# Layer 0's first strips: where shift is computed, and the order of loads and copies around them

## The chip, the core and the metric

The kernel runs on one NeuronCore of one Trainium2 chip. It is one launch. The metric is the time of that launch in microseconds (us) on the device, as the median of several runs. A core has five engines, each with a queue of its own that it works through in order: TensorE (PE, matrix products into PSUM), VectorE (DVE), ScalarE (ACT), GpSimd (POOL) and SyncE (SP), which here only issues DMAs. ACT issues a few DMAs too.

## The reference, cut to what the change touches

Two layers act on one sequence of 1024 tokens with 1024 channels, in float32. Layer 0 is a block-diagonal state-space mixer (S5), layer 1 forgetting attention. Only layer 0's beginning matters here:

```python
def reference(x, c, ...):                       # layer 0
    shift, scale, gate = split(silu(c) @ mod_w + mod_b, 3)
    h = rms(x, norm_g) * (1.0 + scale) + shift
    y = s5_mixer(h, w_in, log_dt, A, B, C, D, w_glu, b_glu, w_out)
    x = x + gate * y                            # then layer 1

def s5_mixer(h, ...):
    u, z = split(h @ w_in, 2)                   # 1024 channels each
    dt = exp(log_dt)
    abar = exp(A_re * dt) * (cos(A_im * dt) + i sin(A_im * dt))
    bb = (abar - 1) / A * B                     # complex, 64 groups
    s[t] = abar * s[t-1] + bb @ u[t]            # per group: 64 states, 16 channels
    y = real(C @ s) + D * u
    y = gelu(y); y = y * sigmoid(y @ w_glu + b_glu); y = y * silu(z)
    return y @ w_out
```

## The kernel before

All of it stands in one function, `trunk`. Products in near-float32 accuracy are made from three products of parts: an operand is split into a high half (a copy in the type fp32r, on ACT, L93) and a low half (the remainder, on DVE, L101), and high times high, low times high and high times low are added in PSUM (`in_part`, L258 to L265).

**Strips.** The product of h with `w_in` is made in strips of 128 output channels. Strip e of u has 1024 x 128 weights, read by `weight_strip` (L83) into the one buffer `w_raw` and split into `w_hi` and `w_lo`, of which there are two each. A strip is made of three chunks of tokens (`CH`): chunk 0 of 512 tokens, chunk 1 of 256, and chunk 2, the short one (`128x258` in the profile), of 256 tokens and two further columns, which hold shift and so give the strip's bias `bi`. In a chunk eight k-tiles by three products are added in a PSUM bank. The part of h without shift is x scaled per channel (`aH`, `aL`, written at L295 and L296 as x arrives); the two shift columns are added to the last tile of tokens (L339, L340). The rms factor is applied to the result: `et` = bank times `q2` (L361, DVE); then `ut` = `et` + `bi` in another order (L378, ACT), and `ut`, of which there is one buffer, is stored to memory as `u_d` (L381, SP).

**What is made first.** `scale` comes with x, k-tile by k-tile (L253 and L288). Strips 0 and 1 (chunks 0 and 1) run with it on PE (`u01`, L310 to L313). Strip 2's weights `raw2` (L315) are split into `w2` in a pool of its own. Shift is silu(c) times `mod_sh`, read as eight tiles `mws` of 512 KB (L324): four of them lie in the ring `xw`, four in the places of `ut`, `bbs`, `x1m` and `x2m`, which so are free only once shift has been computed. The products `psh` (L280 and L283: groups of four products of 32 rows, made side by side) come in two halves of 512 channels, each from all eight tiles. They are copied to `shr` (L332) and turned into columns by eight small products `pm` (L335). Only with these columns can a short chunk start.

**The states' tables.** From A and dt come angles and their sines and cosines (`th`, `ang`, L413 to L437), the powers `pwr`, `pwi` and their signed copies `rvr`, `rvi` (L472, L473), and the coefficients `cr`, `ci`, `cis`. B and C are read twice in two orders: `bb`, `bbs`, `x1m`, `x2m` (L508, L509). `bb` is multiplied by the coefficients, its two halves of partitions are exchanged by DMAs of ACT (`bbs<-bb`, L522), and from `bb`, `bbs` and powers come `wm`, whose transposition `pin` (L595) opens the first group's work on PE. `turn_in` makes `pin`, `taps` the product `pk` (L607), and strips 4 to 7 and those of z are laid among the groups' work.

**What sets the order.** The program is handed to a scheduler which sorts each engine's instructions by a model of their times. `tc.issue_after(m)` adds one constraint: what is written under it comes behind instruction m. Before the change, `mws` come behind the last load of x (L323), the whole chain from `th` on stands behind `last_lo`, the last low half of the shift columns (the gate at L408), and the loads of B and C stand behind the last load of `mws` (L506). The lines that set this for shift are:

```python
psh = [pj.tile([P, HL], F32, name=f"psh{i}", tag="pj") for i in range(2)]
for r in range(2):
    for i in range(2):
        quarters(psh[i], [cs[:, k] for k in range(4 * r, 4 * r + 4)],
                 [t[:, HL * i:HL * i + HL] for t in mws[4 * r:4 * r + 4]], r == 0, r == 1)
```

The tag `pj` is a ring of two PSUM banks that the chunks use too.

## Time and profile before

| what | us |
|---|---|
| median of 3 runs | 1240.18 |
| lowest and highest | 1239.35, 1244.92 |
| the profiled execution's own time | 1235.67 |
| its span, from the first to the last instruction | 1233.9 |
| its time outside the span | 1.77 |

The profile is taken from one execution by the hardware's profiler, and times within it count from the span's start. A row of a timeline holds start, duration, engine, line, operation, output <- inputs, size and count, and in brackets how long the engine had been idle and which instruction ended that. A name without a number stands for all buffers of that name; `u` is a chunk's PSUM bank. The granted clock is the share of full speed at which PE ran. Line numbers are those of the kernel before.

### The profile page before, as it was taken

Reading aid. Unit: us, or ns where it says so; the run is one execution under the profiler, and the core shown is the slowest. Engines: PE = TensorE matmul, PEld = TensorE weight load, DVE = VectorE, ACT = ScalarE, POOL = GpSimd, SP = SyncE. Lnnn points to the kernel's source line nnn. Section 1 sums busy time; section 2 is a strip of 40 time slices with the busy share of each in tenths; the row PEclk is TensorE's granted clock in tenths of the full one; section 3 lists DMA queues with packets and bytes.
Section 4 is the critical chain, followed back from the end, with each engine's and each line's share of the span. In section 5 each row is a group of like instructions: output and inputs, shape, how many; then the busy total and the mean of one; then the engine's idle time right before and its main releaser. Section 6 shows DMA issues by size and latency. Waiting matters only on the chain.

```text
span 1233.9 us, 20697 instructions
## 1 busy us (share of the span) xinstructions
PE 1162.0 (94%) x7594; PEld 1015.9 (82%) x7594; DVE 838.7 (68%) x1708; ACT 606.0 (49%) x1141; POOL 368.5 (30%) x569
## 2 busy tenths in 40 slices
PE   7897999997999998899999999999999999999898
PEld 5586888887878776699989999997888888888686
DVE  7377999894678867856355673448787877887421
ACT  6474667564634422432213352227776777786310
POOL 4000000000000021730043464536675766664100
PEclk8997999998999999999999999999999999999999
DMA  9734556576695697238454159426887969771242
GB/s 353 214 96 119 164 149 174 158 189 192 227 306 184 206 314 259 67 112 259 175 183 171 70 169 190 137 103 153 155 156 135 169 123 172 143 148 27 94 162 77
DMA packets 113333, 205.30 MB, mean 166 GB/s; under 512 B 17072, under 2 KB 58160, under 8 KB 111696
## 3 DMA queue, kind: packets, MB, share of 16 engines
q1 hardware_dynamic: 86272, 161.44, 40.8%
q0 software_dynamic: 24960, 37.75, 17.9%
q10 hardware_dynamic: 2000, 4.79, 1.7%
q8 instruction: 60, 0.98, 0.4%
q14 instruction: 41, 0.34, 0.1%
HBM read 146.47 MB, written 46.20 MB: 156 GB/s over the span
## 4 chain that ended last, share of the span: by engine, by line
PE 56%; DVE 17%; DMA 15%; ACT 4%; issue 4%; SPq 2%; POOL 2%; ACTq 0%; POOLq 0%; DVEq 0%
PE tkps L889 17%; PE zb L112 6%; PE pj_f L112 5%; DMA modw<-modw 5%; PE tp L1081 4%; PE ov L1088 3%; PE u L263 3%; PE ov L1087 3%; PE sp L1048 3%; PE z L263 2%; PE sp L1049 2%; DMA v_d<-vt 2%; PE pj_g L112 2%; PE f L112 2%; DVE modw L132 1%
## 5 line engine op out<-in xcount | busy, mean ns | idle before, releaser
L889 PE MATMUL tkps<-wvh,aH 128*128 128x256 f32 (+1 forms) x768 | 220.7, 287 | 5.7 <-DVE vt L901 2.9
L889 PE MATMUL tkps<-wvh,aL 128*128 128x256 f32 (+1 forms) x768 | 216.8, 282 | 0.0
L889 PE MATMUL tkps<-wvl,aH 128*128 128x256 f32 (+1 forms) x768 | 216.7, 282 | 0.0
L889 PEld LDWEIGHTS tkps<-wvh,aH 128*128 128x128 f32 x768 | 145.1, 189 | 8.2 <-DVE vt L901 3.9
L889 PEld LDWEIGHTS tkps<-wvl,aH 128*128 128x128 f32 x768 | 145.5, 189 | 0.3 <-issue 0.2
L889 PEld LDWEIGHTS tkps<-wvh,aL 128*128 128x128 f32 x768 | 145.0, 189 | 0.3 <-issue 0.2
L1083 ACT ACTIVATE pth<-tp 128x512 fp32r<-128x512 f32 (+1 forms) x192 | 87.1, 488 | 61.0 <-PE ov L1087 35.4
L1056 ACT ACTIVATE pr<-pr,mx 128x128 f32<-128x128 f32 (+7 forms) x128 | 98.9, 773 | 23.0 <-DVE mx L1053 22.5
L1058 POOL TENSOR_SCALAR pr<-pr,sm 128x128 f32<-128x128 f32 (+7 forms) x128 | 96.1, 759 | 41.9 <-DVE sm L1057 41.8
L1084 DVE TENSOR_TENSOR ptl<-tp,pth 128x512 fp32r<-128x512 f32 (+1 forms) x192 | 101.2, 551 | 8.7 <-ACT pth L1083 8.0
L93 ACT ACTIVATE w_hi<-w_raw 128x1024 fp32r<-128x1024 f32 x49 | 51.6, 1054 | 79.9 <-PE pj_f L112 35.8
L1053 DVE CUSTOM_DVE_ANT_0 pr<-sp,fb 128x512 f32<-128x512 f32 (+3 forms) x128 | 72.8, 570 | 22.2 <-PE tp L1081 20.0
L1087 PE MATMUL ov<-pth,vhl 128*128 128x256 f32 x320 | 84.7, 297 | 0.1
L1081 PE MATMUL tp<-ident,pr 128*128 128x128 f32 x576 | 83.1, 273 | 0.0
L912 ACT ACTIVATE hsq<-tkps 128x256 f32<-128x256 f32 x64 | 24.5, 383 | 117.0 <-PE tkps L889 109.8
L1088 PE MATMUL ov<-ptl,vhl 128*128 128x256 f32 x320 | 80.1, 284 | 0.2 <-DVE ptl L1084 0.2
L132 DVE CUSTOM_DVE_ANT_0 modw<-modw,c_b 128x1024 f32<-128x1024 f32 x48 | 58.4, 1220 | 31.2 <-DMA modw<-modw 31.0
L1048 PE MATMUL sp<-kk,qs 128*128 128x256 f32 (+2 forms) x192 | 74.7, 389 | 2.9 <-DVE mx L1053 1.9
L1081 PEld LDWEIGHTS tp<-ident,pr 128*128 128x128 f32 x576 | 65.4, 141 | 7.1 <-POOL pr L1058 0.5
L832 POOL TENSOR_TENSOR sq<-sq,sq 128x512 f32<-128x512 f32 x12 | 19.7, 1645 | 170.8 <-ACT sq L828 170.8
L914 POOL TENSOR_SCALAR hms<-hms 128x4 f32<-128x4 f32 x64 | 16.9, 264 | 174.5 <-DVE hms L913 171.0
L915 POOL TENSOR_TENSOR hms<-hms,nhalf 128x4 f32<-128x4 f32 x64 | 66.4, 1039 | 5.0
(339 smaller groups left out, 3299.8 us busy)
## 6 DMA issues: line engine op xcount, KB each, us to landing
modw<-modw SPq DMA_DIRECT2D x48, 512.0 KB, 5.2
kk<-k_d POOLq DMA_DIRECT2D x32, 512.0 KB, 6.8
wvr<-kvq_w SPq DMA_DIRECT2D x12, 1024.0 KB, 5.3
w_raw<-a_w_in SPq DMA_DIRECT2D x16, 512.0 KB, 4.9
v_d<-vt SPq DMA_DIRECT2D x32, 256.0 KB, 2.8
fb<-f_d SPq DMA_DIRECT2D x16, 512.0 KB, 9.0
vhl<-v_d POOLq DMA_DIRECT2D x16, 512.0 KB, 9.6
qs<-q_d POOLq DMA_DIRECT2D x32, 256.0 KB, 8.4
```

Of the source, the lines that this page charges most:

```text
L112: T.matmul(ps, w[wt][:, k, :], act[at][k][half], start=(k == k0 and n == 0), stop=(k == k1 and n == 2))
L132: V.tensor_tensor_reduce(out=mw, in0=mw, in1=c_b, scale=1.0, scalar=0.0, op0=ALU.mult, op1=ALU.add, accum_out=mod[:, n:n + 1])
L889: T.matmul(ps[:, 0:nv], at, wt[:, k, 0:nv], start=(n == 0), stop=(n == 3 * KT - 1))
L1048: T.matmul(sp[:, 0:wm_], qsl, kk[:, 0, lo:lo + wm_], start=True, stop=False)
L1053: V.tensor_tensor_reduce(out=pr[:, lo:hi], in0=sp[:, 0:w_], in1=fb[:, lo:hi], scale=1.0, scalar=3e38 if m0 is None else m0, op0=ALU.add, o ...
L1056: S.activation(pr[:, 0:nk], pr[:, 0:nk], AF.Exp, scale=-1.0, bias=mx, accum_out=sm)
L1058: G.tensor_scalar(out=pr[:, 0:nk], in0=pr[:, 0:nk], scalar1=sm, scalar2=0.0, op0=ALU.mult, op1=ALU.add)
L1081: T.transpose(out=tp[:, b, :], in_=prs[qi][:, P * (b0 + b):P * (b0 + b) + P], identity=ident)
L1083: S.activation(pth[:, 0:m, dst], tp[:, 0:m, :], AF.Copy)
L1084: V.tensor_tensor(out=ptl[:, 0:m, dst], in0=tp[:, 0:m, :], in1=pth[:, 0:m, dst].bitcast(F32), op=ALU.subtract)
L1087: T.matmul(ov, vhl[:, b, :], pth[:, b - b0, :], start=(b == 0), stop=False)
L1088: end = T.matmul(ov, vhl[:, b, :], ptl[:, b - b0, :], start=False, stop=(b == nb - 1)).ins
```

## The change

The diff has seven edits, all in layer 0's beginning.

- The warm-up products `wu` are 32 instead of 18.
- The load of strip 2's weights stands right behind the last load of x. The eight loads of `mws` follow it one behind another, in the order 4, 5, 6, 7, 0, 1, 2, 3.
- The two halves of shift are made behind chunk 0 and chunk 1 of strip 2, each as a whole from all eight tiles, in a PSUM bank with a tag of its own, `psh`, in the pool `pj0`. There is one such bank, so the second half waits for the copy of the first.
- `pm` and the shift columns come behind both halves.
- Strip 3's weights are read behind the last load of `mws`, in a call of their own, and the loads of B and C come behind that load (`w3_load`).
- The gate of the chain from `th` on is `lo_end`, the last low half of x, instead of `last_lo`.
- The copies of `x1m` and `x2m` come behind strip 3's high half, the products of `bb` and `bbs` behind its low half (`w3_parts`).

```diff
@@ -80,9 +80,11 @@
         fb_t = ctile([NH, 1], "fb_t")
 
 
+        wdma, parts = [], [None] * 2
+
         def weight_strip(src, shape, l_eng=None, pool=None):
             raw = (pool or wpool).tile(shape, F32, name="w_raw", tag="w_raw", bufs=2 if pool else 1)
-            Q.dma_start(out=raw, in_=src)
+            wdma.append(Q.dma_start(out=raw, in_=src).ins)
             hi = wpool.tile(shape, F32R, name="w_hi", tag="w_hi")
             lo = wpool.tile(shape, F32R, name="w_lo", tag="w_lo")
             split(raw, hi, lo, None, l_eng)
@@ -90,15 +92,15 @@
 
         def copy_on(eng, o, i):
             if eng is S:
-                S.activation(o, i, AF.Copy)
+                return S.activation(o, i, AF.Copy)
             elif eng is G:
                 G.tensor_scalar(out=o, in0=i, scalar1=1.0, scalar2=0.0, op0=ALU.mult, op1=ALU.add)
             else:
                 V.tensor_copy(out=o, in_=i)
 
         def split(x, hi, lo, h_eng=None, l_eng=None):
-            copy_on(h_eng or S, hi, x)
-            (l_eng or V).tensor_tensor(out=lo, in0=x, in1=hi.bitcast(F32), op=ALU.subtract)
+            h = copy_on(h_eng or S, hi, x)
+            parts[:] = h, (l_eng or V).tensor_tensor(out=lo, in0=x, in1=hi.bitcast(F32), op=ALU.subtract)
 
 
         def act_tiles(more=0):
@@ -265,7 +267,7 @@
                 return m
 
             wu = pj.tile([P, HL], F32, name="wu", tag="pj")
-            for _ in range(18):
+            for _ in range(32):
                 T.matmul(wu[:, 0:P], onesm, onesm, start=True, stop=True)
             o32 = xp.tile([P, P], F32, name="o32")
             G.memset(o32, 1.0 / 32)
@@ -293,8 +295,8 @@
                 for i in range(2):
                     hi, xs = act[0][k][i][:, 0:HL], xt[:, HL * i:HL * i + HL]
                     S.activation(hi, xs, AF.Copy, scale=s_a[:, k:k + 1])
-                    V.scalar_tensor_tensor(out=act[1][k][i][:, 0:HL], in0=xs, scalar=s_a[:, k:k + 1], in1=hi.bitcast(F32),
-                                           op0=ALU.mult, op1=ALU.subtract)
+                    lo_end = V.scalar_tensor_tensor(out=act[1][k][i][:, 0:HL], in0=xs, scalar=s_a[:, k:k + 1],
+                                                    in1=hi.bitcast(F32), op0=ALU.mult, op1=ALU.subtract).ins
                 sq = xp.tile([P, L], F32, name="sqx", tag="sqx", bufs=4)
                 sq_end = S.activation(sq, xt, AF.Square).ins
                 sqs.append(sq)
@@ -312,33 +314,18 @@
                     for c in range(2):
                         in_part(u01[e][c], w01[e], c, (k,))
             raw2 = wpool.tile([P, KT, P], F32, name="w_raw", tag="w_raw", bufs=1)
-            Q.dma_start(out=raw2, in_=a["a_w_in"][2])
+            with tc.issue_after(last_x):
+                last_w = Q.dma_start(out=raw2, in_=a["a_w_in"][2]).ins
             w2 = [xp.tile([P, KT, P], F32R, name=f"w2{i}", tag=f"w2{i}") for i in range(2)]
             split(raw2, *w2)
 
-            mws = []
-            for k in range(KT):
+            mws = [None] * KT
+            for k in (4, 5, 6, 7, 0, 1, 2, 3):
                 pool, tag = ((s5, "ut"), (s5, "bbs"), (s5, "x1m"), (s5, "x2m"))[k - 4] if k >= 4 else (xp, "xw")
-                mws.append(pool.tile([P, D], F32, name="mws", tag=tag, bufs=7 if pool is xp else 1))
-                with tc.issue_after(last_x):
+                mws[k] = pool.tile([P, D], F32, name="mws", tag=tag, bufs=7 if pool is xp else 1)
+                with tc.issue_after(last_w):
                     last_mod = Q.dma_start(out=mws[k], in_=a["mod_sh"][k])
-            psh = [pj.tile([P, HL], F32, name=f"psh{i}", tag="pj") for i in range(2)]
-            for r in range(2):
-                for i in range(2):
-                    quarters(psh[i], [cs[:, k] for k in range(4 * r, 4 * r + 4)],
-                             [t[:, HL * i:HL * i + HL] for t in mws[4 * r:4 * r + 4]], r == 0, r == 1)
-            shr = xp.tile([P, D], F32, name="shr", tag="sqx", bufs=4)
-            for i in range(2):
-                S.activation(shr[:, HL * i:HL * i + HL], psh[i], AF.Copy)
-            pm = pj0.tile([P, NG], F32, name="pm", tag="dps")
-            for k in range(KT):
-                T.matmul(pm[:, 2 * k:2 * k + 2], shr[:, P * k:P * k + P], o32[:, 0:2], start=True, stop=True)
-            for k in range(KT):
-                hi, b = act[0][k][1][:, HL:], vec["modb"][:, k:k + 1]
-                m = pm[:, 2 * k:2 * k + 2]
-                S.activation(hi, m, AF.Identity, bias=b)
-                last_lo = V.scalar_tensor_tensor(out=act[1][k][1][:, HL:], in0=m, scalar=b, in1=hi.bitcast(F32),
-                                                 op0=ALU.add, op1=ALU.subtract).ins
+                    last_w = last_mod.ins
             with tc.issue_after(sq_end):
                 S.preload_act_table_set("natural_log_exp_and_others")
             vx = xp.tile([P, L], F32, name="vx")
@@ -397,15 +384,37 @@
                     yield m
 
             u2 = []
+            shr = xp.tile([P, D], F32, name="shr", tag="sqx", bufs=4)
             for c in range(2):
-                u2.append(u_norm(chunk(w2, c, "u2")[0], c, xp))
+                ps, m = chunk(w2, c, "u2")
+                u2.append(u_norm(ps, c, xp))
+                with tc.issue_after(m):
+                    psh = pj0.tile([P, HL], F32, name=f"psh{c}", tag="psh")
+                    for r in range(2):
+                        quarters(psh, [cs[:, k] for k in range(4 * r, 4 * r + 4)],
+                                 [t[:, HL * c:HL * c + HL] for t in mws[4 * r:4 * r + 4]], r == 0, r == 1)
+                S.activation(shr[:, HL * c:HL * c + HL], psh, AF.Copy)
+            pm = pj0.tile([P, NG], F32, name="pm", tag="dps")
+            for k in range(KT):
+                T.matmul(pm[:, 2 * k:2 * k + 2], shr[:, P * k:P * k + P], o32[:, 0:2], start=True, stop=True)
+            for k in range(KT):
+                hi, b = act[0][k][1][:, HL:], vec["modb"][:, k:k + 1]
+                m = pm[:, 2 * k:2 * k + 2]
+                last_hi = S.activation(hi, m, AF.Identity, bias=b).ins
+                last_lo = V.scalar_tensor_tensor(out=act[1][k][1][:, HL:], in0=m, scalar=b, in1=hi.bitcast(F32),
+                                                 op0=ALU.add, op1=ALU.subtract).ins
             for e in range(U_FIRST):
-                for _ in u_strip(e, *((w01[e], u01[e]) if e < 2 else (w2, (), u2) if e == 2 else ())):
+                if e == 3:
+                    with tc.issue_after(last_mod.ins):
+                        w3 = weight_strip(a["a_w_in"][3], [P, KT, P])
+                    w3_parts = [p.ins for p in parts]
+                for _ in u_strip(e, *((w01[e], u01[e]) if e < 2 else (w2, (), u2) if e == 2 else (w3,))):
                     pass
+            w3_load = wdma[-1]
 
 
             gate = ExitStack()
-            gate.enter_context(tc.issue_after(last_lo))
+            gate.enter_context(tc.issue_after(lo_end))
 
             th = tmp.tile([P, 8, NG], F32, name="th")
             mul(th[:, 0], aim, dt)
@@ -503,21 +512,23 @@
             bbs = s5.tile([P, NG, GC], F32, name="bbs", tag="bbs")
             x1m = s5.tile([P, NG, GC], F32, name="x1m", tag="x1m")
             x2m = s5.tile([P, NG, GC], F32, name="x2m", tag="x2m")
-            with tc.issue_after(last_mod.ins):
+            with tc.issue_after(w3_load):
                 for o, i0, i1 in ((bb, "B_re", "B_im"), (bbs, "B_im", "B_re"), (x1m, "C_re", "C_im"), (x2m, "C_im", "C_re")):
                     Q.dma_start(out=o[0:64], in_=a[i0])
                     Q.dma_start(out=o[64:128], in_=a[i1])
-            S.activation(x1m, x1m, AF.Copy, scale=sg_pm)
-            S.activation(x2m, x2m, AF.Copy, scale=-1.0)
 
             cis = tmp.tile([P, NG], F32, name="cis")
             S.activation(cis, ci, AF.Copy, scale=sg_mp)
+            with tc.issue_after(w3_parts[0]):
+                S.activation(x1m, x1m, AF.Copy, scale=sg_pm)
+                S.activation(x2m, x2m, AF.Copy, scale=-1.0)
             shb = [P, NG // 2, GC]
             for gs in (slice(0, 32), slice(32, 64)):
                 crb, cib = (t[:, gs].unsqueeze(2).broadcast_to(shb) for t in (cr, cis))
-                mul(bbs[:, gs], bbs[:, gs], cib)
-                mul(bb[:, gs], bb[:, gs], crb)
-                tt(bb[:, gs], bb[:, gs], bbs[:, gs], ALU.add)
+                with tc.issue_after(w3_parts[1]):
+                    mul(bbs[:, gs], bbs[:, gs], cib)
+                    mul(bb[:, gs], bb[:, gs], crb)
+                    tt(bb[:, gs], bb[:, gs], bbs[:, gs], ALU.add)
                 for hh in range(2):
                     S.dma_start(out=bbs[64 * hh:64 * hh + 64, gs], in_=bb[64 - 64 * hh:128 - 64 * hh, gs])
 
```

How the order of the instructions moves is seen at three places. The first is PE between strip 1 and strip 2. `msy` are the rms sums, `u_1_190` and `u_0_525` are banks of chunks, `psh` shift's halves, `pm` the columns' bank. Before, all of shift's products and half of `pm` stand ahead of strip 2's first chunk:

```order
L309 MATMUL msy_344<-mq,o_210 128x512
L280 MATMUL psh_465<-mws,cs 32x512
L283 MATMUL psh_465<-mws,cs 32x512 x3
L280 MATMUL psh_466<-mws,cs 32x512
L283 MATMUL psh_466<-mws,cs 32x512 x3
L280 MATMUL psh_465<-mws,cs 32x512
L283 MATMUL psh_465<-mws,cs 32x512 x3
L280 MATMUL psh_466<-mws,cs 32x512
L283 MATMUL psh_466<-mws,cs 32x512 x3
L335 MATMUL pm<-o_210,shr 128x2 x4
L263 MATMUL u_0_525<-aH_0_150,w_445 128x512
```

Now strip 2's chunk 0 comes straight behind strip 1, and the first half, `psh_521`, stands within its chunk 1 (`u_1_531`):

```order
L265 MATMUL u_1_531<-aH_1_161,w_459 128x256
L282 MATMUL psh_521<-mws,cs 32x512
L285 MATMUL psh_521<-mws,cs 32x512 x3
L282 MATMUL psh_521<-mws,cs 32x512
L285 MATMUL psh_521<-mws,cs 32x512 x3
L265 MATMUL u_1_531<-aL_1_177,w_459 128x256
```

and the second, `psh_558`, behind that chunk, followed by all eight `pm` and the short chunks of strips 0 and 1 (`u_2_595`, `u_2_633`):

```order
L265 MATMUL u_1_531<-aH_1_165,w_460 128x256
L282 MATMUL psh_558<-mws,cs 32x512
L285 MATMUL psh_558<-mws,cs 32x512 x3
L282 MATMUL psh_558<-mws,cs 32x512
L285 MATMUL psh_558<-mws,cs 32x512 x3
L399 MATMUL pm<-o_224,shr 128x2 x8
L265 MATMUL u_2_595<-aH_1_151,w_hi 128x258
L265 MATMUL u_2_633<-aH_1_151,w_hi 128x258
```

So the first half moved behind chunk 0 and most of chunk 1, the second stands eight chunk products further on, and the columns come in one piece. The short chunks of strips 0 and 1, which before came mostly one after the other, are now laid into each other to their end.

The second place is SP's queue behind the last load of x (`xt`). `fb_t` and `dsk` are small constants. Before:

```order
L288 DMA xt<-xT 128x1024
L324 DMA mws<-mod_sh 128x1024 x4
L508 DMA bb<-B_re 64x1024
L315 DMA w_raw<-a_w_in 128x1024
L509 DMA bb<-B_im 64x1024
L324 DMA mws<-mod_sh 128x1024
L527 DMA fb_t<-f_bias 16x1
L324 DMA mws<-mod_sh 128x1024
L528 DMA dsk<-D 128x16
L324 DMA mws<-mod_sh 128x1024 x2
L85 DMA w_raw<-a_w_in 128x1024
L508 DMA x2m<-C_im 64x1024
```

Now:

```order
L290 DMA xt<-xT 128x1024
L318 DMA w_raw<-a_w_in 128x1024
L327 DMA mws<-mod_sh 128x1024 x8
L538 DMA fb_t<-f_bias 16x1
L539 DMA dsk<-D 128x16
L87 DMA w_raw<-a_w_in 128x1024
L517 DMA bb<-B_re 64x1024
L518 DMA bb<-B_im 64x1024
L517 DMA x2m<-C_im 64x1024
L518 DMA x2m<-C_re 64x1024
L517 DMA bbs<-B_im 64x1024
L518 DMA bbs<-B_re 64x1024
```

The load of strip 2's weights moved ahead of all of `mws`, `bb` moved out from among them, and the loads into `mws`' former places follow strip 3's weights.

The third place is ACT from strip 3's split on: `x1m` and `x2m` are C's tiles, `ut` the strips' outputs, `bbs<-bb` the exchange of halves. Before, `x2m` and `x1m` stood right behind `shr` and ahead of the shift columns:

```order
L332 ACTIVATE shr<-psh_465 128x512
L332 ACTIVATE shr<-psh_466 128x512
L511 ACTIVATE x2m<-x2m 128x1024
L510 ACTIVATE x1m<-x1m,sg_pm 128x1024
L339 ACTIVATE aH_1_151<-pm,vecs 128x2
L339 ACTIVATE aH_1_153<-pm,vecs 128x2
```

Now they stand behind strip 3's split and ahead of strip 0's `ut`, and the exchanges are issued on either side of strip 1's:

```order
L403 ACTIVATE aH_1_165<-pm,vecs 128x2
L95 ACTIVATE w_hi<-w_raw 128x1024
L523 ACTIVATE x1m<-x1m,sg_pm 128x1024
L524 ACTIVATE x2m<-x2m 128x1024
L365 ACTIVATE ut<-et,bi 128x32x8
L365 ACTIVATE ut<-et,bi 128x64x8
L365 ACTIVATE ut<-et,bi 128x32x8
L95 ACTIVATE w_hi<-w_raw 128x1024
L533 DMA bbs<-bb 64x512 x2
L365 ACTIVATE ut<-et,bi 128x32x8
L365 ACTIVATE ut<-et,bi 128x64x8
L365 ACTIVATE ut<-et,bi 128x32x8
L533 DMA bbs<-bb 64x512 x2
```

## The prediction

> **What bounds the kernel now.** I read the page first, then a table of windows cut where TensorE (PE) changes its work, then the waits of the first 140 us, then single rows. The page says that PE is the engine to follow: busy 94% of the span, and most of the chain that ended last.
>
> ```profile
> span 1233.9 us, 20697 instructions
> PE 1162.0 (94%) x7594; PEld 1015.9 (82%) x7594; DVE 838.7 (68%) x1708; ACT 606.0 (49%) x1141; POOL 368.5 (30%) x569
> PE 56%; DVE 17%; DMA 15%; ACT 4%; issue 4%; SPq 2%; POOL 2%; ACTq 0%; POOLq 0%; DVEq 0%
> ```
>
> The windows (from:to, length, busy time of PE, PEld, DVE, ACT, POOL with counts, granted clock, DMA share, GB/s) show where PE stands still:
>
> ```profile
> 24.94:41.89 16.95, 16.92 (x92) 12.02 (x92) 10.43 (x18) 11.55 (x17) 0.00 (x0) 1.00 1.03 320
> 41.89:47.02 5.13, 0.01 (x1) 0.03 (x1) 4.05 (x6) 3.25 (x6) 0.00 (x0) 0.95 1.01 373
> 47.02:52.93 5.91, 5.91 (x41) 2.22 (x41) 0.96 (x2) 1.19 (x2) 0.00 (x0) 0.75 0.03 12
> 52.93:62.47 9.54, 9.54 (x58) 8.27 (x57) 0.00 (x0) 1.87 (x2) 1.00 (x2) 1.00 0.74 167
> 62.47:77.45 14.98, 12.22 (x97) 11.79 (x97) 10.14 (x30) 8.85 (x23) 0.00 (x0) 1.00 0.21 71
> 77.45:94.87 17.42, 17.38 (x96) 14.70 (x96) 14.87 (x45) 13.10 (x31) 0.00 (x0) 1.00 0.48 143
> 94.87:103.79 8.92, 0.00 (x0) 0.03 (x1) 4.19 (x10) 3.54 (x7) 0.11 (x1) 0.66 0.76 194
> 103.79:111.38 7.59, 7.32 (x38) 6.54 (x39) 6.78 (x10) 0.80 (x2) 0.00 (x0) 0.50 0.01 3
> 106.00:150.00 44.00, 43.69 (x317) 39.84 (x318) 37.85 (x54) 26.27 (x42) 0.74 (x2) 0.94 0.46 119
> ```
>
> From 24.94 to 41.89 PE is full: strips 0 and 1. Then it stands for 5.13 us, does shift's products and the pm columns at a reduced clock (mean 0.75) in 5.91, strip two in 9.54, and so on to a second hole of 8.92 behind which the clock is 0.50. After 106 it is full again (43.69 of 44.00). So a microsecond taken from PE's path before 111 should come off the end. The waits (waiter, released by; total, times, longest) name the holes:
>
> ```profile
> PE pin L595 <- DVE wm L197: 8.9, 1, 8.9
> PE psh L280 <- DMA mws<-mod_sh: 5.1, 1, 5.1
> PE u L263 <- ACT w_hi L93: 5.1, 2, 4.9
> PE u L263 <- DVE aL L340: 2.0, 1, 2.0
> ```
>
> **The change part by part.** *Warm-ups, 18 to 32.* They fill part of the 4.9 us before the first strip's weights. By 24.94 PE has caught up with its inputs (16.92 of the next 16.95 us busy), so an earlier or faster start only moves idle time; I take 0, with ends of 1.0 gained and 0.2 lost.
>
> The Trainium skill, "TensorE: Matmul & The Clock Gate", Part 1, says that the throttled clock is the default and that sustained activity releases it; by it the fuller start could return half of the products run at half clock there. The trace bears out the lower clock, not that its end is on the path, so this adds nothing.
>
> *Third strip's weights ahead of shift's.* Both land under the full stretch up to 41.89; shift's last 512 KB is no longer needed at 41.89, but when psh0 runs, some 7 us later.
>
> ```profile
> 38.34 8.54 DMA mws<-mod_sh
> 50.18 0.59 PE L280 MATMUL psh<-mws,cs 128*32 128x512 f32 x1
> 50.61 0.59 PE L280 MATMUL psh<-mws,cs 128*32 128x512 f32 x1
> 52.20 0.60 ACT L332 ACTIVATE shr<-psh 128x512 f32<-128x512 f32 x1 [0.28 <-PE psh L283]
> 56.97 0.95 PE L335 MATMUL pm<-o,shr 128*128 128x2 f32 x8
> 57.77 0.71 PE L263 MATMUL u<-aH,w 128*128 128x512 f32 x2
> 64.51 0.36 PE L263 MATMUL u<-aH,w_hi 128*128 128x258 f32 x1 [2.03 <-DVE aL L340]
> 70.73 0.36 PE L263 MATMUL u<-aH,w 128*128 128x258 f32 x1 [0.20 <-DVE et L361]
> 77.45 0.47 PE L263 MATMUL u<-aH,w_hi 128*128 128x512 f32 x1 [0.53 <-DVE bi L375]
> ```
>
> In the trace the last load landed at 38.34 + 8.54 = 46.88 and that stall was the 5.13. Without B's 512 KB between them I expect them some 4 us earlier; even at 46.88 they are in time.
>
> *Shift behind the chunks of strip two.* From 41.89 PE goes straight on: strip two's two chunks are 9.54 less the 0.80 that pm took inside (56.97 to 57.77), 8.74. Shift's eight groups of four go at 0.43 each at full clock (50.18 to 50.61): 3.44. That makes 41.89 + 8.74 + 3.44 = 54.07. Behind it stand the copy of the second half (0.60), pm (0.95), the first aH/aL columns and their handoffs: 2.4 by the sum of such rows, first short chunk at 56.5. The ends are 55.9 (1.8, just these rows) and 58.0: on ScalarE (ACT) that copy now stands among copies of the powers that wait for VectorE (DVE). psh1 has to wait until the first half's copy has left the one bank: eight products of the chunk stand between the halves, about 1 us of PE, against 0.60 and a handoff, so nothing, or up to the 1.0 that the later end holds if that copy is late on ACT. Before, the short chunk began at 64.51, so **8.0 us** are gained here.
>
> *The clock behind it.* The stretch from 53.3 to 56.7 is one of the throttle's 3.41 us steps, and PE has about 1.9 us of work in it. The trace has such steps of both outcomes:
>
> ```profile
> 224.03:227.44 3.41, 1.79 (x20) 1.59 (x21) 3.41 (x6) 2.32 (x6) 0.00 (x0) 1.00 0.86 247
> 227.44:230.85 3.41, 3.41 (x13) 2.96 (x12) 3.31 (x4) 1.72 (x4) 0.00 (x0) 0.50 0.31 42
> 292.30:295.71 3.41, 1.91 (x17) 1.71 (x15) 0.89 (x1) 0.00 (x0) 0.00 (x0) 1.00 1.08 402
> 295.71:299.12 3.41, 0.00 (x0) 0.00 (x0) 0.31 (x1) 1.54 (x2) 0.00 (x0) 1.00 0.76 175
> ```
>
> A step with 1.79 busy is followed by half clock, one with 1.91 is not. A halved step loses up to 1.7; 1.9 lies between the rows, part of it a modelled end, so I take 1.3, with ends 0 and 1.7. The pair of short chunks then ends at 56.5 + 6.2 (64.51 to 70.73) + 1.3 = 64.0, where it ended at 70.73: 6.7 gained so far.
>
> The Trainium skill, same page and part, gives the fall to half clock only after an idle window of about 3.4 us; by it this 1.3 would not arise. The rows at 224.03 and 227.44 speak against it (1.79 of 3.41 busy, and yet half clock next).
>
> *B and C behind strip three's weights; their copies behind its split.* This adds waits.
>
> ```profile
> 52.09 0.47 SPq L508 DMA_DIRECT2D x2m<-C_im  x1
> 55.86 5.70 DMA x1m<-C_im
> 61.66 1.15 ACT L510 ACTIVATE x1m<-x1m,sg_pm 128x1024 f32<-128x1024 f32 x1 [3.15 <-DMA x1m<-C_im]
> 68.76 1.06 ACT L93 ACTIVATE w_hi<-w_raw 128x1024 fp32r<-128x1024 f32 x1 [0.23 <-PE u L263]
> 70.61 2.38 ACT L378 ACTIVATE ut<-et,bi 128x256 f32<-128x256 f32 x3 [0.80 <-DVE et L361]
> 73.02 2.98 DMA u_d<-ut
> 84.31 4.89 DMA u_d<-ut
> ```
>
> SyncE (SP) issues the six loads into tiles that held shift's weights once psh1 is done, at 54.07, where it began at 52.09: the last lands near 63.5 (55.86 + 5.70 + 2). ACT's queue from 64.0 is strip three's high half (1.06, its buffer held by strip 0 until the pair ends), x1m (1.15), x2m (about the same) and then ut of strip 0 (2.38), from 67.2 to about 69.5. Queued behind it is DVE's et for strip 1, which needs the buffer that ut gives back and which frees a PSUM bank for PE: strip three's short chunk starts near 68.6 where PE is free at 66.9, **1.7 lost**. Next ut of strip 0 is stored (2.98), strip four's split and two DMA issues stand on ACT ahead of strip 1's ut, which begins near 73.9; PE waits some 3.1 more for it. PE reaches strip three's first wide chunk at 64.0 + 6.0 of its own work (70.73 to 77.45 less 0.20 and 0.53 of waits) + 4.8 = 74.8, where it was 77.45. The ends for the 4.8: 2 (only x1m and x2m count) and 8.5.
>
> *The chain of powers starts with the last x column* rather than shift's, near 38 instead of 67. Its work is on DVE and ACT beside full PE stretches (10.43 and 11.55 busy of 16.95), and a second Sin table load between the copies costs ACT about as much as one handoff; neither is late. What it brings is at pin:
>
> ```profile
> 94.39 2.46 ACTq L522 DMA_DIRECT2D bbs<-bb  x4
> 94.92 7.32 DMA bbs<-bb
> 102.36 0.62 DVE L197 TENSOR_TENSOR tm<-bbs,rvi 128x448 f32<-128x448 f32 x1 [4.66 <-DMA bbs<-bb]
> ```
>
> PE's 8.92 hole is the chain: swapped copies issued from 94.39, landed at 102.24, tm, wm, pin at 103.79. Now the products stand on DVE right behind strip three's lower half (66.2), and the order puts the second pair of copies on ACT behind strip 1's ut, at about 77: landed by 84.7, wm by 86. PE needs it at 74.8 + 17.42 = 92.2. So the hole goes, with 6 us to spare: PE at pin 103.79 − 92.2 = **11.6 us** earlier in all. With the hole goes the half clock behind it: half of 7.32 busy is **3.66**. What is late next is small (the first group's vps and decay products follow on the same engines): −0.3.
>
> Sum: 11.6 + 3.66 − 0.3 = 15.0. The 11.6 are 8.0 at the first short chunk, −1.3 for its clock, −4.1 for the new waits (4.8 less the 0.73 that stood there) and 8.9 for the hole, to the rounding. The profiled execution takes 1235.67 (span 1233.9 and 1.77 around it), so 1220.7 by its measure. The median of the runs is 1240.18, 4.5 above it; the gain is a difference within one execution, so I take it from the median: **1225.2**.
>
> **The rivals.** *The new waits are covered.* If ut of strip 0 stays ahead, PE comes to pin at 92.2 − 4.8 = 87.4, still behind wm's 86: 16.4 + 3.66 − 0.3 = 19.8, near 1220.4. For it: ACT is busy 8.85 of 14.98 there; against it: x1m waited 3.15 for its load, and the load comes later.
>
> *The change doesn't do what it says at pin.* If the products or ACT's issues slip, wm comes behind 92.2: from 6 us of slip on the hole opens again, at 15 it is whole. For it: ut, two splits and both pairs stand in one ACT queue there, and the copies took 7.32 to land; against it: 6 us. If the whole 8.92 and its 3.66 stay, 15.0 − 12.6 = 2.4: near 1237.8, no change.
>
> *Slower: the single ut buffer.* Each strip's ut can be rewritten only when its store has landed, and on SP that store stands behind the load of a later strip's weights, which waits for the one w_raw buffer. Before, the chain's stores went out at 73.02 and 84.31 with one between them, 5.6 us a round, against 17.42 / 1.5 = 11.6 of PE work for a strip. Should a store wait for the split before it, a round would be a strip long and more. It decides from a round of 14.6, where over five strips (3 to 7) 5 × 3.0 eats the 15.0; slower by 0.5% needs 15.8. At 16.6 it is 5 × 5.0 = 25, less 15.0: near 1250. Against it: twice its present round is still below PE's strip.
>
> **How the numbers follow.** Forecast, a gain of about 8 to 18: 0.68. Waits covered: 0.17. Hole stays: 0.10. Slower: 0.05. The low end takes the covered waits with the early short chunk (0.6), no halved step (1.3) and the warm-ups' 1.0: 22.7, 1217. The high end takes 58.0 for the short chunk (1.5), 8.7 of waits (3.7) and 1.7 for the clock (0.4), a gain of 9.4 and 1230.8, and goes halfway from there to the returned hole: 1234. A measurement of this kernel can tell about 0.5% (6.2 us) from no change; faster by more 0.85 (the first two), within 0.10, slower 0.05.
>
> **What would show it.** PE runs from strip 1's last product into strip two without a hole at 42; the first short chunk near 56.5; the throttle's step behind it at 0.50; waits of PE on et or ut near 67 and 72, 5 us together (none, if they are covered); pin near 92 with no wait for wm and a clock of 1.00 behind it; all later stages shifted alike. It would be wrong if psh0 still waited for its weights, if pin waited for wm, or if a stage after 111 gave back what was won.

## The result and the profile after

The changed kernel takes 1223.31 us (median of 4 runs, 1221.77 to 1224.37) against 1239.76 before, run beside it: ratio 0.9863, 95% interval 0.9826 to 0.9900. The forecast was 1225.2 in a range of 1217 to 1234, faster. In a second series (run e5 below) the ratio is 0.9845 (0.9809 to 0.9882). One of e4's ten executions below took 1605.09 us, at a granted clock of 0.654; e4's median counts it, its ratio doesn't.

The page of the changed kernel, span, busy shares and the engines' shares of the chain that ended last:

```profile
span 1220.5 us, 20752 instructions
PE 1167.8 (96%) x7622; PEld 1022.3 (84%) x7622; DVE 843.8 (69%) x1708; ACT 609.6 (50%) x1143; POOL 369.0 (30%) x569
PE 65%; DVE 14%; DMA 9%; issue 5%; ACT 5%; SPq 1%; POOL 1%; POOLq 0%; DVEq 0%; ACTq 0%
```

PE's share of the chain rose from 56% to 65%, that of DMA fell from 15% to 9%: waits for transfers went. The windows, cut where PE changes its work, columns as before:

```profile
24.90:41.39 16.49, 16.45 (x90) 11.89 (x91) 12.54 (x22) 13.59 (x24) 0.00 (x0) 1.00 1.03 406
41.39:53.99 12.60, 12.60 (x85) 8.49 (x83) 11.84 (x39) 7.31 (x15) 0.00 (x0) 1.00 0.25 55
53.99:56.40 2.41, 2.06 (x21) 1.86 (x17) 2.02 (x8) 2.24 (x8) 0.24 (x1) 1.00 0.37 97
56.40:64.04 7.64, 7.63 (x48) 7.42 (x48) 2.85 (x13) 3.53 (x14) 0.76 (x2) 0.78 0.76 175
64.04:73.56 9.52, 6.25 (x48) 5.93 (x49) 9.01 (x18) 7.19 (x9) 0.00 (x0) 1.00 0.45 141
73.56:90.55 16.99, 16.98 (x96) 14.79 (x97) 7.90 (x15) 7.97 (x16) 0.11 (x1) 1.00 0.70 212
90.55:111.35 20.80, 20.80 (x166) 18.62 (x165) 17.97 (x24) 13.91 (x22) 0.00 (x0) 1.00 0.40 108
```

Strip two and shift run without a hole from 41.39 to 53.99 (12.60 busy of 12.60). The short chunks start at 56.40 and run at a mean clock of 0.78. From 64.04 to 73.56 PE stands 3.3 us. Then it is full through pin at 90.55 and behind it, at full clock: the hole of 8.92 and the half clock are gone. PE's rows at the starts of these stretches, with what ended the idle time ahead:

```profile
56.40 0.51 PE L265 MATMUL u<-aH,w_hi 128*128 128x258 f32 x2 [0.35 <-ACT aH L403]
64.47 0.36 PE L265 MATMUL u<-aH,w 128*128 128x258 f32 x1 [0.43 <-DVE et L348]
69.33 0.36 PE L265 MATMUL u<-aH,w_hi 128*128 128x258 f32 x1 [1.75 <-DVE bi L362]
73.56 0.47 PE L265 MATMUL u<-aH,w_hi 128*128 128x512 f32 x1 [1.10 <-DVE bi L362]
90.55 0.60 PE L606 MATMUL pin<-ident,wm 128*128 128x128 f32 x4
133.71 0.43 PE L618 MATMUL pk<-moa,bb 128*32 128x128 f32 x8 [1.92 <-ACT moa L592]
```

| landmark on PE, us | before | forecast | after |
|---|---|---|---|
| first short chunk | 64.51 | 56.5 | 56.40 |
| strip two's short chunk | 70.73 | 64.0 | 64.47 |
| strip three's short chunk | | 68.6, wait 1.7 | 69.33, wait 1.75 |
| strip three's first wide chunk | 77.45 | 74.8 | 73.56 |
| pin of the first group | 103.79 | 92.2 | 90.55 |
| last pk of layer 0's groups | 273.9 | 15.0 earlier | 258.8, 15.1 earlier |
| span | 1233.9 | 15.0 shorter | 1220.5, 13.4 shorter |

So the gain stands whole at the end of layer 0's groups, and 1.7 us of it are missing at the end of this execution. How much that says is seen in the runs.

### The profile page after: what moved, and what is told of

Read it like the earlier page. It is cut to its first block, busy times and chain, and to the rows that moved or that the text cites. A ratio compares the mean times of both kernels' runs of the same rounds, so it can differ in the third digit from the quotient of the medians.

```text
span 1220.5 us, 20752 instructions
## 1 busy us (share of the span) xinstructions
PE 1167.8 (96%) x7622; PEld 1022.3 (84%) x7622; DVE 843.8 (69%) x1708; ACT 609.6 (50%) x1143; POOL 369.0 (30%) x569
## 4 chain that ended last, share of the span: by engine, by line
PE 65%; DVE 14%; DMA 9%; issue 5%; ACT 5%; SPq 1%; POOL 1%; POOLq 0%; DVEq 0%; ACTq 0%
PE tkps L900 16%; PE zb L114 7%; PE pj_g L114 6%; PE pj_f L114 5%; PE tp L1092 5%; PE u L265 4%; PE ov L1099 3%; DMA v_d<-vt 3%; PE ov L1098 3%; PE sp L1059 3%; DMA modw<-modw 3%; PE sp L1060 3%; PE z L265 3%; PE f L114 2%; PE pj_o L114 1%
## 5 line engine op out<-in xcount | busy, mean ns | idle before, releaser
L900 PE MATMUL tkps<-wvl,aH 128*128 128x256 f32 (+1 forms) x768 | 217.0, 283 | 0.0
L95 ACT ACTIVATE w_hi<-w_raw 128x1024 fp32r<-128x1024 f32 x49 | 51.7, 1055 | 77.2 <-PE pj_f L114 35.8
L1064 DVE CUSTOM_DVE_ANT_0 pr<-sp,fb 128x512 f32<-128x512 f32 (+3 forms) x128 | 72.8, 570 | 21.9 <-PE tp L1092 20.0
```

The costliest lines, as they stand in the source:

```text
L900: T.matmul(ps[:, 0:nv], at, wt[:, k, 0:nv], start=(n == 0), stop=(n == 3 * KT - 1))
L1064: V.tensor_tensor_reduce(out=pr[:, lo:hi], in0=sp[:, 0:w_], in1=fb[:, lo:hi], scale=1.0, scalar=3e38 if m0 is None else m0, op0=ALU.add, o ...
```

## The experiments

The kernels ran in four series, each beside the kernel before, whose median was 1239.76, then 1237.26 (e1 to e4), 1237.64 (e5 to e8) and 1237.68 (e9 to e12). The start of strip two differs from run to run by up to 2.75 us, and by 1.8 between kernels that are alike up to there (changed and e8). I therefore read one measure from each profile besides the time: from the end of the last `msy` product (the start of strip two) to the start of the last `pk` product of layer 0's groups. The column before it is the part of that up to `pin` of the first group, the one behind it what is left of the span. "Halved" counts the throttle's steps of 3.41 us at a granted clock of 0.50 in the measured stretch and, behind the plus sign, in the rest of the span.

| run | strip two starts | to pin | measure | rest of span | halved | median us | ratio to before, 95% |
|---|---|---|---|---|---|---|---|
| before | 41.89 | 61.9 | 232.0 | 960.0 | 6 + 3 | 1239.76 |  |
| changed | 41.39 | 49.2 | 217.4 | 961.7 | 2 + 7 | 1223.31 | 0.9863 (0.9826 to 0.9900) |
| e5, changed again | 41.69 | 48.0 | 217.4 | 957.7 | 1 + 2 | 1218.32 | 0.9845 (0.9809 to 0.9882) |
| e1, 18 warm-ups | 43.07 | 50.8 | 218.9 | 963.0 | 2 + 6 | 1226.35 | 0.9902 (0.9870 to 0.9935) |
| e2, gate late | 42.77 | 55.2 | 224.3 | 958.6 | 5 + 3 | 1227.74 | 0.9914 (0.9886 to 0.9943) |
| e3, gate only | 44.14 | 59.6 | 229.0 | 962.0 | 5 + 6 | 1235.09 | 0.9985 (0.9960 to 1.0011) |
| e4, shift first | 42.80 | 55.4 | 223.2 | 965.8 | 4 + 7 | 1230.63 | 0.9936 (0.9915 to 0.9956) |
| e6, copies later | 42.20 | 46.3 | 214.2 | 960.7 | 1 + 4 | 1220.04 | 0.9857 (0.9823 to 0.9891) |
| e7, shift inside | 42.35 | 48.6 | 215.8 | 961.3 | 2 + 4 | 1221.35 | 0.9863 (0.9834 to 0.9893) |
| e8, both | 43.19 | 46.1 | 213.1 | 966.2 | 1 + 7 | 1225.33 | 0.9903 (0.9872 to 0.9933) |
| e9, shift first, shr first | 42.13 | 47.4 | 215.5 | 963.6 | 1 + 7 | 1221.35 | 0.9868 (0.9842 to 0.9895) |
| e10, gate, shr first | 41.73 | 58.8 | 227.7 | 963.4 | 4 + 6 | 1233.45 | 0.9977 (0.9957 to 0.9997) |
| e11, products later | 42.75 | 51.7 | 218.2 | 961.5 | 2 + 5 | 1223.75 | 0.9886 (0.9861 to 0.9910) |
| e12, old order of loads | 42.47 | 52.7 | 221.0 | 957.6 | 3 + 5 | 1226.98 | 0.9914 (0.9888 to 0.9939) |

The measure is the same to 0.1 us in the two executions of the changed kernel, but that is in part chance: at `pin` they stand 1.2 apart, and from `pin` to the last `pk`, where no edit stands, the runs e1 to e12 take 166.5 to 169.4. The rest of the span, where no edit stands either, lies anywhere from 957.6 to 966.2, and it goes with its halved steps: 957.7 to 961.3 with 2 to 4 of them, 961.7 to 966.2 with 6 or 7 (with 5 once 957.6, once 961.5). The 1.7 us missing above fit that: 3 halved steps before, 7 in the first execution after. Below, differences of 3 us and more are read from the measure, smaller ones only where the way to `pin` shows them too; the time bears only the large ones. The expectations of e9 and e10 give the measure of e3, e4 and e5 as 228.7, 222.9 and 217.0; these end 0.3 earlier, at the last `pk` product of `moa`, the table at the last of all.

**The first four: which edit brings it.**

e1 takes the warm-ups back:

```diff
-            for _ in range(32):
+            for _ in range(18):
                 T.matmul(wu[:, 0:P], onesm, onesm, start=True, stop=True)
```

> The changed kernel with 18 warm-up products instead of 32. My account (PE has caught up with its inputs by 24.9 either way): the first short chunk starts at 56.4 within 0.5 us, pin of the first group at 90.5 within 0.7, the time at 0.986 to 0.988 of before. Rival (the earlier full clock is worth what it shows): everything from 25 us on is 1.0 to 2.6 us later.

The landmarks missed by 3 to 4 us, first short chunk 60.38, pin 93.8, and the time, 0.9902, is above its 0.988. Two things make that up. Strip two starts at 43.07, in the runs with 32 warm-ups at 41.39 to 43.19, in the three others with 18 (before, e3, e10) at 41.73 to 44.14: within the spread of both. The measure is 1.5 longer; most of that is a wait of 1.66 of the second psh for shr's copy on the one bank (the scheduler placed that copy later in this build), which is ACT's order and not the clock. So what the warm-ups do to the start, up to some 1.7 us, stays open in the spread of the starts; within the stretch that is measured no effect of theirs shows.

e2 holds the chain of angles and powers back again:

```diff
-            gate.enter_context(tc.issue_after(lo_end))
+            gate.enter_context(tc.issue_after(last_lo))
```

> The changed kernel with the chain of angles and powers held behind the last low half of the shift columns again, as before the change. My account: the chain starts at 61.4 instead of 38, and since it took 36.5 us from its start to the last wm before the change, wm comes near 98 while PE is at pin by 90.5: the hole at pin is back with some 7 us, the half clock behind it with 3.7, together 10 to 12 us lost, ratio near 0.996. Rival (the early chain only loads DVE and ACT beside the strips, and the gain is all from shift): less than 3 us lost.

```profile
98.01 0.63 PE L606 MATMUL pin<-ident,wm 128*128 128x128 f32 x4 [1.86 <-DVE wm L199]
```

```profile
75.48:82.31 6.83, 6.03 (x14) 4.79 (x15) 6.50 (x28) 5.18 (x12) 0.00 (x0) 0.50 0.36 142
99.38:102.79 3.41, 3.41 (x21) 3.03 (x22) 3.31 (x6) 0.10 (x1) 0.00 (x0) 0.50 0.00 0
```

wm comes at 98 as worked out, and pin 7.5 later than in the changed kernel (1.4 of it strip two's later start). But PE itself reaches pin only at 96.2 (it waits 4.7 for et ahead of it, and two steps at half clock begin in the longest of these waits, 3.44), so the hole is 1.86, and one halved step stands behind it instead of the stretch at half clock up to 111.38 before the change. The measure is 6.9 longer, which is neither 10 to 12 nor the rival's under 3; the gate is worth that, in one profile, with all else changed.

e3 makes the gate's edit alone, on the kernel before (`lo_end` set at the low halves of x, and `issue_after(lo_end)` at the gate).

> The kernel before with one edit, the chain of angles and powers behind the last low half of x. My account: PE still stands 5.1 us for shift's weights and the short chunks still start at 64.5, but the hole at pin (8.9) and the half clock behind it (3.7) go: about 12 us gained, ratio near 0.990; so the rest of the change is worth only 3 to 5 us net of the waits that it adds. Rival (the two need each other, because the copies of B wait for tiles that shift holds): under 5 us gained.

This missed: the measure is 3.0 shorter than before, the time the same (0.9985). The rival's number held, though not by its reason: PE waits 7.19 on shr, as the first of the next rows shows, and with the wait the clock falls to half for three steps, 55.04 to 65.28. The other rows are from e4.

e4 puts shift back ahead of strip two, in the two banks of `pj`, with all else as changed:

```diff
+            psh = [pj.tile([P, HL], F32, name=f"psh{i}", tag="pj") for i in range(2)]
+            for r in range(2):
+                for i in range(2):
+                    quarters(psh[i], [cs[:, k] for k in range(4 * r, 4 * r + 4)],
+                             [t[:, HL * i:HL * i + HL] for t in mws[4 * r:4 * r + 4]], r == 0, r == 1)
...
             for c in range(2):
                 ps, m = chunk(w2, c, "u2")
                 u2.append(u_norm(ps, c, xp))
-                with tc.issue_after(m):
-                    psh = pj0.tile([P, HL], F32, name=f"psh{c}", tag="psh")
```

> The changed kernel with shift's products back ahead of strip two's chunks and in the chunks' banks, all else as changed (the order of the loads too). My account: the last of shift's weights lands near 43.8 (issued 32.4, 11.4 to land), so PE stands 2.4 us at 41.4 instead of 5.1, the columns are made beside the chunks, and the short chunks start near 57.5, 1.1 later than 56.4, without the half clock behind them: the time within 1.5 us of the changed kernel, because the order of the loads alone takes most of the hole away. Rival (the place behind the chunks is what takes the hole away): short chunks at 60 or later and 3 to 5 us lost.

PE in e3:

```profile
57.47 1.87 PE L335 MATMUL pm<-o,shr 128*128 128x2 f32 x8 [7.19 <-ACT shr L332]
```

PE, the window of half clock, and ACT in e4:

```profile
53.99 1.87 PE L339 MATMUL pm<-o,shr 128*128 128x2 f32 x8 [6.32 <-ACT shr L336]
```

```profile
51.30:61.54 10.24, 7.55 (x22) 6.29 (x23) 5.92 (x27) 5.09 (x16) 0.00 (x0) 0.50 0.46 100
```

```profile
52.23 0.32 ACT L482 ACTIVATE rvr<-pwr 128x64 f32<-128x64 f32 x1 [0.65 <-DVE pwr L199]
53.05 0.41 ACT L483 ACTIVATE rvi<-pwi,sg_mp 128x64 f32<-128x64 f32 x1 [0.50 <-DVE pwi L199]
53.36 0.58 ACT L336 ACTIVATE shr<-psh 128x512 f32<-128x512 f32 x1
```

My account missed again by time (measure 5.8 over the changed kernel's, expected within 1.5), but not at the weights: psh starts at 44.03, with no wait for its loads (0.77 of idle time, ended by `q2x` on ACT). Its products end at 47.7; then the copy shr stands on ACT behind the Sin, its table load and copies of powers that wait one by one for DVE, and pm, at the head of PE's queue, waits 6.32. With the wait comes half clock, 7.55 us of work at 0.50. In e3 the same costs 7.19, with one wait of 3.11 on a power and two more table loads of 1.28 on ACT in it. An early chain and an early shift collide on ACT: a wait on DVE's powers is handed through ACT's queue to PE.

**The next four: the waits that the change adds.**

e5 is the changed kernel again.

> The changed kernel itself, as the measure for the runs beside it on this chip: short chunks at 56.4, strip three's short chunk at 69.3 behind a wait of 1.75, its wide chunk at 73.6, pin of the first group at 90.5, all within 1.5 us of start, ratio 0.984 to 0.990.

It lands as expected; from strip two's short chunk to pin its landmarks stand 1.1 to 1.2 us nearer to the start of strip two, because the step at half clock is missing (last section).

e6 moves the two copies on ACT and the products on DVE (in the changed kernel's lines, `ut_ins` and `et_ins` keep the instructions of `u_strip`):

```diff
-            with tc.issue_after(w3_parts[0]):
+            with tc.issue_after(ut_ins[0]):
                 S.activation(x1m, x1m, AF.Copy, scale=sg_pm)
...
-                with tc.issue_after(w3_parts[1]):
+                with tc.issue_after(et_ins[1]):
                     mul(bbs[:, gs], bbs[:, gs], cib)
```

> The changed kernel with x1m's and x2m's copies behind strip 0's ut on ACT, and the products of bb and bbs behind strip 1's et on DVE. My account: the wait of 1.75 ahead of strip three's short chunk is made by the two together (ut of strip 0 stands behind the copies, and et of strip 1 behind four products), so it goes; the wait ahead of its wide chunk stays, since ut of strip 1 still needs strip 0's store (about 3 us) and the split of strip four. Wide chunk 1.0 to 1.9 us earlier against the start of strip two than in the changed kernel, and the time 1 to 2 us better. Rival (the wait only moves to the next chunk): under 0.3 us at the wide chunk.

e11 moves the products alone (the second hunk).

> The changed kernel with the products of bb and bbs behind strip 1's et on DVE alone, x1m's and x2m's copies where the change has them. e6 moved both. My account (both hold et): the wait of 1.75 ahead of strip three's short chunk falls to 0.5 to 1.0. Rival (DVE's products alone make it): to 0.3 or less; other rival (ACT's copies alone): it stays above 1.4.

The rows of DVE in the changed kernel that it is about, strip three's low half, four products, then et of strip 1 and bi of strip two:

```profile
65.23 1.21 DVE L103 TENSOR_TENSOR w_lo<-w_raw,w_hi 128x1024 fp32r<-128x1024 f32 x1
66.36 0.68 DVE L199 TENSOR_TENSOR bbs<-bbs,cis 128x512 f32<-128x512 f32 x1
...
68.16 0.68 DVE L199 TENSOR_TENSOR bb<-bb,cr 128x512 f32<-128x512 f32 x1
68.77 0.41 DVE L348 TENSOR_TENSOR et<-u,q2x 128x256 f32<-128x256 f32 x1
69.10 0.15 DVE L362 COPY bi<-u 128x1 f32<-128x1 f32 x1
```

ACT's ut of strip 0, which gives et its buffer back, stands behind the two copies and starts at 66.66; the first of its three parts is done by 67.4. From there to 68.77 et is held by the products. PE's rows in e11 and, last, in e6:

```profile
69.39 0.36 PE L265 MATMUL u<-aH,w_hi 128*128 128x258 f32 x1 [0.43 <-DVE et L350]
75.87 0.49 PE L265 MATMUL u<-aH,w_hi 128*128 128x512 f32 x1 [3.37 <-DVE et L350]
```

```profile
71.53 0.47 PE L265 MATMUL u<-aH,w_hi 128*128 128x512 f32 x1 [1.41 <-DVE bi L366]
```

With the products moved (e11) the wait of 1.75 falls to 0.43, between "the products alone" (0.3 or less) and my 0.5 to 1.0: most of it was theirs. But the next wait grows from 1.10 to 3.37, and pin comes 2.5 later (51.7 behind the start of strip two, 49.2 in the changed kernel): the wait only moved, and grew. With ACT's copies moved as well (e6) the first wait is gone from PE's rows, the second is 1.41, and the wide chunk stands 29.3 behind the start of strip two instead of 31.0 (e5); the measure is 3.2 shorter, 1.7 of it up to pin (against e5). The time doesn't show it (0.9857 against 0.9845).

e7 takes both halves of shift into chunk 0 and the columns into chunk 1, in an order written out:

```diff
+            at = {(0, 5): lambda: shift_half(0), (0, 7): lambda: shift_half(1), (1, 1): lambda: columns(0), (1, 5): lambda: columns(1)}
...
+                for k in range(KT):
+                    with tc.issue_after(m) if m is not None else ExitStack():
+                        m = in_part(ps, w2, c, (k,))
+                    if (c, k) in at:
+                        with tc.issue_after(m):
+                            m = at[c, k]()
...
+                with tc.issue_after(last_lo) if m == 4 else ExitStack():
...
+            with tc.issue_after(last_hi):
+                for j in range(7):
```

`shift_half` makes one half and its copy, `columns` four of the pm products. The last step of the powers stands behind the shift columns on DVE, and the copies rvr, rvi and cis behind them on ACT. e8 is e6 and e7 together.

> The changed kernel with both halves of shift within chunk 0 of strip two (behind its k 5 and k 7), the pm columns within chunk 1, and the shift columns ahead of the copies of powers on ACT, so that nothing stands between chunk 1 and the short chunks. My account: first short chunk 2 us earlier against the start of strip two, no throttled step behind it (1.3), so strip two's short chunk 3 to 4 us earlier and the time about 3 us better. Rival (the chain of powers, now behind the columns, decides): pin waits for wm, under 1 us better.

> The two edits before together. My account: 4 to 5 us better than the changed kernel. Rival (the chain to wm or the store of ut decides by then): no better than the better of the two.

Strip two's short chunk in e7 stands 21.3 behind the start of strip two, in e5 21.9, in the first profile 23.1; the measure is 1.6 better than the changed kernel's in e7, half of what I expected, and 4.3 in e8, as expected. At pin less is left: e7 stands at 48.6 (e5 48.0), e8 at 46.1, which e6 alone reaches with 46.3. So a gain of e7's edit isn't shown, and e8's rival, no better than the better of the two, isn't refuted. In e7 the next wait has grown (2.82 for et ahead of strip three's short chunk), and pin doesn't wait for wm, which was the rival. Neither is faster by time, and e8, the best by the measure, took 1225.33: its rest of the span is 966.2 against e5's 957.7. The clock shows a part of that, in the same 150 us of e5, then e8, then the first execution of the changed kernel:

```profile
450.00:600.00 150.00, 138.87 (x963) 126.61 (x962) 95.27 (x142) 48.55 (x77) 37.97 (x23) 1.00 0.53 177
```

```profile
450.00:600.00 150.00, 139.02 (x934) 126.73 (x933) 92.34 (x136) 46.48 (x76) 35.79 (x22) 0.95 0.49 165
```

```profile
450.00:600.00 150.00, 138.67 (x921) 125.78 (x920) 95.65 (x138) 47.03 (x75) 36.77 (x23) 0.95 0.49 164
```

PE is as busy in all three, but the granted clock is 1.00 in e5 and 0.95 in e8, with 934 instructions done against 963. A mean of 0.95 is four of the 3.41 us steps at half clock. The changed kernel's first execution has the same four without any edit of e8's, so these steps aren't e8's doing. They aren't all of the difference either: behind the last `pk` both have 7 halved steps, and e8's rest of the span is 4.5 longer. What makes that stays open; all four runs of e8 lie between 1224.2 and 1228.4.

**The last four: is the place needed, or the order on ACT, or the loads?**

e9 is e4 with ACT's order repaired; e10 is e3 with the same, and C's copies and the exchanges behind the shift columns:

```diff
-                S.activation(shr[:, HL * i:HL * i + HL], psh[i], AF.Copy)
+                shr_end = S.activation(shr[:, HL * i:HL * i + HL], psh[i], AF.Copy).ins
...
+            with tc.issue_after(shr_end):
+                S.activation(sn, th[:, 0], AF.Sin)
+                S.activation(cs, tb[:, 0], AF.Sin, scale=-1.0, bias=hpi)
...
+            with tc.issue_after(shr_end):
+                for j in range(7):
+                    S.activation(rvr[:, :, j], pwr[:, :, 6 - j], AF.Copy)
```

The copies `turn` and `cis` stand under the same line.

> The kernel of e4 (shift ahead of strip two, in the chunks' banks, all else as changed) with the Sin, the angles' and the powers' copies on ACT held behind shift's two copies. Measure: from the end of the last msy product (start of strip two) to the last pk product of layer 0's groups; it is 232.0 before, 217.4 and 217.0 changed, 222.9 in e4. My account after e4 (the only harm of the old place is that shift's copies stand behind the early chain on ACT, and pm behind them on PE): no wait of pm over 1.5 us, short chunks 15 to 16 us behind the start of strip two, measure 216 to 218.5. Rival (the place behind the chunks matters by itself): measure 221 or more.

> The kernel of e3 (before, with the early chain alone) with the same order on ACT, shift's copies ahead of the chain's, and C's copies and the exchanges' issues behind the shift columns. Measure as in e9: 228.7 in e3. My account (e3 lost its gain on ACT's queue alone): the hole at pin and the half clock behind it go, and pm doesn't wait for shr: measure 216 to 220, 1.0% below before. Rival (the loads and the place are needed too): 224 or more.

ACT and PE in e9:

```profile
46.19 0.60 ACT L336 ACTIVATE shr<-psh 128x512 f32<-128x512 f32 x1 [1.63 <-PE psh L285]
47.02 0.60 ACT L336 ACTIVATE shr<-psh 128x512 f32<-128x512 f32 x1 [0.23 <-PE psh L285]
```

```profile
43.29 0.59 PE L282 MATMUL psh<-mws,cs 128*32 128x512 f32 x1 [0.70 <-DMA mws<-mod_sh]
46.86 1.05 PE L339 MATMUL pm<-o,shr 128*128 128x2 f32 x8
```

The 6.32 is gone, psh waits 0.70 for its last load, and the measure is 215.5, no longer than with shift behind the chunks (217.4; to pin 47.4, there 49.2 and 48.0); the time is the changed kernel's (0.9868). So the place behind the chunks and the bank of its own aren't what makes the gain. With the new order of the loads and shr ahead of the chain on ACT, shift can stay where it was.

e10 says that the early chain and this order aren't enough on the kernel before:

```profile
46.81 1.03 PE L280 MATMUL psh<-mws,cs 128*32 128x512 f32 x1 [5.08 <-DMA mws<-mod_sh]
```

It still waits 5.08 for the last of shift's weights, at the old order of the loads, then runs half of psh at half clock (rows of 1.03 to 1.06 against 0.59). pin no longer waits for wm, but PE comes to it only at 100.5: et waits 3.97 ahead of strip three's wide chunk. The measure, 227.7, is on the rival's side. e10 lacks more than the order of shift's loads, though: strip three's weights and the loads of B and C are at their old places too, so the 12.2 us to e9 aren't the price of one edit.

e12 keeps the new place and takes back the loads' order:

```diff
-            with tc.issue_after(last_x):
-                last_w = Q.dma_start(out=raw2, in_=a["a_w_in"][2]).ins
+            Q.dma_start(out=raw2, in_=a["a_w_in"][2])
...
-            for k in (4, 5, 6, 7, 0, 1, 2, 3):
+            for k in range(KT):
...
-                with tc.issue_after(last_w):
+                with tc.issue_after(last_x):
```

> The changed kernel with the loads as before: shift's weights in the order 0 to 7, strip two's weights where the scheduler puts them among them. My account: shift no longer waits for its weights in either order, since it is made 8 us later; but strip two's weights land near 40 and are split by 43 to 44, so PE stands 1 to 2.5 us ahead of strip two: measure (as in e9) 218 to 220. Rival (the order of the loads is what takes the 5.1 away): psh waits for its weights, 221 or more. Other rival (no effect, as the prediction had it): 217.0 to 217.5.

```profile
42.87 0.50 PE L265 MATMUL u<-aH,w 128*128 128x512 f32 x1 [0.39 <-ACT w L95]
58.42 1.29 PE L397 MATMUL pm<-o,shr 128*128 128x2 f32 x8 [1.09 <-ACT shr L394]
```

psh doesn't wait for its weights, so in the new place their order doesn't matter. Strip two's weights cost 0.39 and not 1 to 2.5, yet the measure is 3.6 longer. All of that is there by strip two's short chunk: 1.1 up to the end of psh (0.75 of it waits, for the weights and for `vx`), 1.5 from there to the first short chunk (1.09 a wait of pm for shr), and 1.0 in the pair of chunks, which runs in two steps at half clock:

```profile
59.08:65.91 6.83, 6.48 (x31) 6.39 (x31) 2.29 (x10) 2.97 (x12) 1.00 (x2) 0.50 0.79 178
```

So 221.0 meets the number of the rival, but not its reason. The order of the scheduler's other instructions shifts with the loads; how much is due to that and how much to the loads was not tried apart. Not tried alone at all are the old places of strip three's weights and of the loads of B and C.

## Why the prediction was right, point by point

- *Shift no longer stalls PE, 8.0 us at the first short chunk.* Right, 64.51 to 56.40, with 0.5 of it from the earlier start of strip two (41.39 against 41.89), which the change doesn't explain. Its terms held: 12.60 from the start of strip two to the last psh (forecast 54.07 less 41.89, 12.18), then 2.41 (forecast 2.4).
- *Both weights land under cover.* Right in what it gave. e4, e9, e10 and e12 show why: either edit, new place or new order, takes the 5.1 us hole away. They are substitutes, which the forecast saw only from one side.
- *The throttled step, 1.3.* Right in size for the first profile, in part by luck. The pair of chunks with its following wait took 8.07 there, in e5 6.92 for the same instructions: 1.15. It came in the one and not in the other, so the ends 0 and 1.7 were the better part of that term. The step that the forecast looked at, 53.3 to 56.7, has the borders of the execution before; in those of the changed kernel they lie elsewhere, and its 1.9 us of work counted pm in full (last section).
- *Waits of 1.7 and 3.1.* The first is 1.75, in its place. Its cause was half seen: not only ut behind ACT's copies, but et and bi behind four products on DVE (e11 took 1.3 of it away by moving these alone). The second was 1.10, mis-sized by 2.0: strip four's split and the first issues went ahead of strip 1's ut as forecast, but that ut began at 72.23 and not near 73.9. Strip 0's ut had ended 0.7 earlier than forecast, and what ut waited for last was its store (0.94 behind the split). That is most of why pin came 1.65 earlier than worked out.
- *The hole at pin, 8.92, and the half clock behind it, 3.66.* Both gone: no wait ahead of pin, clock 1.00 in 90.55:111.35. e2 confirms the gate's part by taking it back: pin at 98.01 with a wait again, of 1.86, and a halved step behind it.
- *A second Sin table load, about one handoff; chain and load not late.* The table load took 1.28 us. Here the forecast was right for the change as it is, and e3 and e4 show how narrowly: the chain makes shr late by 6 to 7 us when shift is early. The early chain alone was worth 3.0 of the 12.6 that I gave it in e3. With shift early it pays only in an order that keeps shr from standing behind it on ACT.
- *What is late next, −0.3.* Mis-sized: pin was 13.24 early and 3.66 of half clock were saved, 16.9, of which 15.1 were left at the last pk. 1.92 of it is one new wait, pk for moa's copy on ACT at 133.71 (0.3 in all before). The late first waits that I had priced too high and this one that I hadn't made out about cancel; the sum of 15.0 is better than its terms, which is luck. The medians moved by 16.5 and, in e5's series, by 19.3 (1237.64 to 1218.32), the profiled spans by 13.4: the rest of the span, which the forecast doesn't reach, decides within that.
- *Warm-ups, 0.* Not contradicted (e1), but up to some 1.7 us can't be told from the spread of the starts.
- *The rivals.* Waits covered: no, 2.85 of them stayed. The hole stays: no. The single ut buffer: stores go out at 68.87 and 74.45, rounds of 5.6, far from the 14.6 from which it would decide. (The high end of the range writes 8.7 of waits; its bound and the 3.7 taken off are those of 8.5.)

## What to carry to other kernels

When a chain of small dependent operations is started earlier, look at each engine's queue for who stands behind it: a copy of 0.6 us that an early chain holds for 6 is a stall on the engine that needs it, and an edit that earns 3.0 us alone, and nothing by time (e3), can be worth 6.9 together with edits that keep that copy out of its way (e2). Two edits that remove the same hole (a new place, an earlier load) must be tried apart before either is credited. Where the far part of a program spreads by 8 us, read the edit from landmarks near it, look at the granted clock before blaming an edit for the rest (e8), and don't call a version better by landmarks faster before its time says so (e6 to e8).
